# A hybrid decoder layer in float32: the order of three groups of weight loads and the run length of two stores

## The chip, the cores and the metric

The kernel runs on one core of a Trainium2 chip. The metric is the device time of one execution in microseconds (us): the median over several runs. Each run also has a span, from the first to the last instruction, and a granted TensorE clock. The engines are named as in the profile: PE (TensorE, matmuls), PEld (its weight loads), DVE (VectorE), ACT (ScalarE), POOL (GpSimd) and SP (SyncE, which here only issues transfers). ACT and POOL issue transfers too. An "L" with a number is a line of the kernel.

## The reference

One layer of a decoder, all in float32, for 2048 tokens of width 1024: a mixer (retention and pooling heads), cross-attention into 256 memory tokens, and a gated MLP, each with a norm in front and a residual add behind. What matters here, cut to the core:

```python
mem_n = rmsnorm(mem, mem_norm_g)
h = rmsnorm(x, mix_norm_g[l])
q, k, v, g, u = jnp.split(h @ w_in[l], [R, 2 * R, 3 * R, 4 * R], axis=-1)
y_ret = jax.nn.silu(g) * head_rmsnorm(retention(q, k, v, positions), ret_gn_g[l])
y_pool = pool_mixer(u, pool_w[l], pool_scale[l])
x = x + jnp.concatenate([y_ret, y_pool], axis=-1) @ w_out[l]
x = x + cross_attn(rmsnorm(x, xa_norm_g[l]), mem_n, xa_wq[l], xa_wkv[l], xa_wo[l])
x = x + conv_glu_ffn(rmsnorm(x, ffn_norm_g[l]), ffn_w_up[l], ffn_conv_w[l], ffn_conv_b[l], ffn_w_down[l])
...
# in cross_attn
q = h @ wq
k, v = jnp.split(mem_n @ wkv, 2, axis=-1)
s = (q k^T) * (XA_HEAD_DIM ** -0.5); p = softmax(s); o = p v
return o @ wo
# in pool_mixer: 4 groups of 128 channels
out = jnp.einsum('bsgc,gcd->bsgd', pooled, w); return out * scale
```

## The kernel before

**Precision.** Each float32 operand is split into a high part (float32r, rounded by an ACT copy) and a low part (the difference, on DVE): `split` (L256), or `pairs` (L285) for a block of weights in two halves. A product is three matmuls, high x high, high x low and low x high: `passes` (L269, matmuls at L271 to L273). So before any matmul of a block stand its load, two ACT copies (L259, or L262 with a gain) and two DVE subtractions (L243, L251).

**Buffers.** Raw blocks of 128 x 1024 land in five slots used in turn, `raws` (three in the tile R, two in tiles S). `new_raw` takes the slot that has been free longest and frees it in the program at once, so the next load into it waits for the splits of the block before. Halves go to `prs` (tile Q, and regions of G or E lent to it for a time). Slots in Z, eight of 128 x 1024, are taken with `Z.take(n)`, which picks the aligned group that was freed longest ago. TensorE's results go to PSUM banks (`mm`, five of them).

**Order of work.** The program is written in the order of its stages. A scheduler then fixes the order on each engine and each queue from that order and its own timing of the program; each engine then takes its list in that order and waits where an operand isn't there. Side work is a generator, `folded_weights` (L439), of which `folded(n)` (L2010) runs n steps at a place. Its steps:
1. Eight for the keys of the memory tokens and eight for their values (`project`, L480; the values are kept in the DRAM tensor Vd).
2. Four, one for each head: rows of `xa_wq` (wqT, two blocks of 512 KB, `row_pairs` at L495) times the keys give a score matrix, stored to the DRAM tensor Md (L548, L501).
3. One that loads poolT and the first rows of the output projection's pool half (wout_p, L497).
4. Two steps with one "pool product" each, then one with two more and the loads of Vd: pool weights times rows of wout_p, four groups g, each copied from two PSUM banks (L592) into a slot of Z and stored to the DRAM tensor WPd (L594) in runs of 128 values (512 B). The groups 2 and 3 take again the slots of groups 0 and 1.
5. Eight "half items" (`at` 0 to 7, L612): the values of a head times a half of its rows of `xa_wo` (two loads, L569, for each head; taken two half items ahead), copied with a scale (L633) and stored to the DRAM tensor VWd (L634), two stores of 256 KB a half item, in runs of 512 B.

**Stages for the first 1024 tokens.** The loop at L2021 runs steps 1 and 2 beside the loads of tokens (L658, L669). In its last four turns it also loads the weights of the retention values, w_v, 512 KB each (`value_weights`, L730, called at L2035 ahead of `folded(1)`), two into arena 0 (G, where the operands of the memory tokens had been) and two into arena 1 (E). `values` (L739) then uses them, and `quarter_sums` and `head_projections` follow; step 3 and the first two pool products lie in the last items of the head projections (L1886, L1888). After those come `folded(2)` (L2079: the last two pool products, then half item 0) and `folded(1)` for each remaining step of the last head's retention (L2081). Then the eight "output units" begin (L2116). Unit n loads wout_r[n] (L2118) and WPd[n] (L2119) into the two halves of a raw slot; the second half of its matmuls needs the latter. After the units 0, 1 and 2 run 1, 2 and 4 further steps (L2128).

Of the kernel before, what the change touches and what calls it, by code (L numbers as in the profile page):

```python
# [11 lines left out]
AF = mybir.ActivationFunctionType  # L12
# [3 lines left out]
P = 128  # L16
D = 1024
KT = D // P
SEQ = 2048
NMEM = 256  # L20
T = 1024
SUB = 512
# [114 lines left out]
def trunk(ctx, tc, xT, xR, memT, pos, w_qkgu, w_v, wkv, wqT, wo, wout_r, wout_p, poolT, w_up, w_dn, vecs, consts, outT):  # L137
    nc = tc.nc
    pe, act, dve, pool, sp = nc.tensor, nc.scalar, nc.vector, nc.gpsimd, nc.sync
# [11 lines left out]
    G = cp.tile([P, 28 * T], F32R, tag="G", name="G")  # L151
    X = G[:, : 2 * KT * T].rearrange("p (j t) -> p j t", t=T)

    def new_e(dtype):
        return Arena(cp.tile([P, 4 * T], dtype, tag="E", name=nm("E")), 0, 4, T)
# [4 lines left out]
    B = Joined(Arena(G, 16 * T, 12, T), new_e(F32R))  # L160

    def new_z(dtype):
        return Arena(cp.tile([P, 8 * T + 4 * EDGE], dtype, tag="Z", name=nm("Z")), 0, 8, T)

    Z = new_z(F32)
# [53 lines left out]
    VWd = drp.tile([KT, P, KT, P], F32, tag="VWd", name="VWd")  # L219
# [3 lines left out]
    WPd = drp.tile([KT, P, 4, P], F32, tag="WPd", name="WPd")  # L223

    def mmps():
        return mmp.tile([P, SUB], F32, tag="mm", name=nm("mm"))
# [42 lines left out]
    def passes(ps, lhs, rhs, start, stop, more=False):  # L269
        (lh, ll), (rh, rl) = lhs, rhs  # L270
        pe.matmul(ps, lh, rh, start=start, stop=False, skip_group_check=more)  # L271
        pe.matmul(ps, lh, rl, start=False, stop=False, skip_group_check=more)  # L272
        latest[0] = pe.matmul(ps, ll, rh, start=False, stop=stop, skip_group_check=more)  # L273
# [30 lines left out]
    def lend(region):  # L304
        for i in range(region.n):
            prs.freed.append(len(prs.one))
            prs.one.append(Arena(region.arena.t, region.arena.base + (region.first + i) * T, 1, T))

    def reclaim(region):
        for _ in range(region.n):  # L310
            prs.one.pop()
            prs.freed.remove(len(prs.one))
        region.free()
# [125 lines left out]
    def folded_weights():  # L439
# [18 lines left out]
        for k in range(KT):  # L458
            h, j = divmod(k, 4)
# [6 lines left out]
        rn = smp.tile([P, 4], F32, tag="rnm", name="rnm", bufs=1)[:, :2]  # L466
# [13 lines left out]
        def project(n):  # L480

            if n < 2:
                hs = first[0] if n == 0 else pairs(first[1])
            else:
                hs = pairs(load_tile(wkv[n]))
            if n % 2 == 0:
                bank[:] = [mmps()]
            at = n % 2 * NMEM
            ps = bank[0][:, at : at + NMEM]
            for k in range(KT):  # L490
                w = [hs[k // 4][:, i, (k % 4) * P : (k % 4 + 1) * P] for i in range(2)]
                passes(ps, w, (mh[:, k], ml[:, k]), k == 0, k == KT - 1)
            return ps

        def row_pairs(src):  # L495
            raw = new_raw()
            sp.dma_start(raw, src)  # L497
            return pairs(raw)
# [5 lines left out]
        def tiles4(d, nh, k):  # L504
            return d[4 * nh : 4 * nh + 4, :, k, :].rearrange("n p c -> p n c")
# [3 lines left out]
        ps = [project(n) for n in range(2)]  # L509
        sp.dma_start(cs_t, consts)  # L510
        memory_norm()
        for n in range(KT):
            if n > 1:
                ps.append(project(n))
            if n % 2:
                for at in (n - 1, n):
                    t = TT.take()
# [6 lines left out]
        for n in range(KT):  # L524
            ps.append(project(KT + n))
            if n % 2:
                del ps[:]
                t = TT.take()
# [7 lines left out]
        for h in range(HEADS):  # L536
            dp = [row_pairs(wqT[(2 * h + dt) * P : (2 * h + dt + 1) * P, :]) for dt in range(2)]
            for k2 in range(KT // 2):
                ps = mmps()
                for j in range(2):  # L540
                    for dt in range(2):
                        k = 2 * k2 + j
                        w = [dp[dt][k // 4][:, i, k % 4 * P : (k % 4 + 1) * P] for i in range(2)]
                        passes(ps[:, j * NMEM : (j + 1) * NMEM], w, (kp4[:, 2 * h + dt, 0], kp4[:, 2 * h + dt, 1]), dt == 0, dt == 1)
                t = TT.take()
                for j in range(2):
                    k = 2 * k2 + j
# [18 lines left out]
        def rows(h):  # L566
            got = [raws.take() for _ in range(2)]
            for dt, r in enumerate(got):
                sp.dma_start(r.f, wo[(2 * h + dt) * P : (2 * h + dt + 1) * P, :])  # L569
            return got  # L570
# [7 lines left out]
                    r.free()  # L578
            return out

        vp4, held = G[:, 8 * T : 12 * T].rearrange("p (n i m) -> p n i m", i=2, m=NMEM), []
        ended = []
        for g in range(4):
            u = ahead.pop(0)
            if g < 2:
                held.append(Z.take())
            t = held[g % 2]
            for nh in range(2):
                ps = mmps()
                lh = [pw.r[:, i * SUB + g * P : i * SUB + (g + 1) * P] for i in range(2)]  # L590
                passes(ps, lh, [u[nh][:, i] for i in range(2)], True, True)
                done = act.activation(t.f[:, nh * SUB : (nh + 1) * SUB], ps, AF.Copy)  # L592
            ended.append(done)
            act.dma_start(WPd[:, :, g, :].rearrange("n p c -> p n c"), t.f.rearrange("p (n c) -> p n c", n=KT))  # L594
            if g > 1:
                t.free()
            if g == 0:
                prs.freed.sort(key=lambda i: i < 3)
                ahead.append(row_pairs(wout_p[3]))
                got = rows(0)  # L600
            if g < 2:
                yield
# [9 lines left out]
        for at in range(2 * HEADS):  # L612
            h, nh = divmod(at, 2)
            dp = ahead
            if at == 2:
                reclaim(spare)
                spare = [Arena(G, at_g * T, 2, T).take(2) for at_g in (12, 6)]
                for r in spare:
                    lend(r)
                prs.freed.sort(key=lambda i: i < 3)  # L620
            if at + 1 < 2 * HEADS:
                with tc.issue_after((ended[-1] if at else ended[2]).ins):
                    ahead = halved(got, 1 - nh)
                if not nh and h + 1 < HEADS:
                    got = rows(h + 1)
            t = Z.take()
            for mt in range(2):
                ps = mmps()
                for dt in range(2):
                    lh = [vp4[:, 2 * h + dt, i, mt * P : (mt + 1) * P] for i in range(2)]  # L630
                    passes(ps, lh, [dp[dt][:, i] for i in range(2)], dt == 0, dt == 1)
                out = t.f[:, mt * SUB : (mt + 1) * SUB]
                ended.append(act.activation(out, ps, AF.Identity, scale=rn[:, mt : mt + 1]))  # L633
                act.dma_start(tiles4(VWd, nh, 2 * h + mt), out.rearrange("p (n c) -> p n c", n=4))  # L634
            t.free()
            yield
        for r in reversed(spare):
# [92 lines left out]
    def value_weights(kp, home=None):  # L730
        raw = new_raw()
        sp.dma_start(raw.rearrange("p (k n) -> p k n", k=2), w_v[2 * kp : 2 * kp + 2].rearrange("k p n -> p k n"))
        u = (home or B).take(2)
        for i in range(2):
            r = raw[:, i * SUB : (i + 1) * SUB]
            split(r, u.r[:, i * T : i * T + SUB], u.r[:, i * T + SUB : (i + 1) * T])
        return u
# [1272 lines left out]
    def folded(n):  # L2010
        for _ in range(n):
            next(todo, None)
# [4 lines left out]
    room, wv = [Z.take() for k in range(KT)], []  # L2017
# [3 lines left out]
    for n in range(1, 2 * KT + HEADS):  # L2021
        if n <= KT:
            load_tokens(0, n - 1, room)
        if 1 < n <= KT + 1:
            token_squares(0, n - 2, room, token_sums)
        if n == KT + 2:
            rn, _ = token_norm(token_sums[:, :KT])
        if n in xs_at:
            load_x_wide(xs_at[n], room)
        if n == 2 * KT:  # L2030
            reclaim(spare)
            spare = B.arenas[0].take(4)
            lend(spare)
        if 2 * KT <= n < 2 * KT + 4:
            wv.append(value_weights(n - 2 * KT, B.arenas[(n - 2 * KT) // 2]))  # L2035
        folded(1)
    reclaim(spare)
    for b in range(NB):

# [33 lines left out]
        if b:  # L2073
            parts = [next(heads)]
        else:
            slow[0], paced[0], spacing[0] = False, True, 7
            for _ in heads:
                pass
            folded(2)  # L2079
            for _ in behind[0]:  # L2080
                folded(1)  # L2081
            paced[0] = False
        mix = got[1]

# [31 lines left out]
        for n in range(first, KT):  # L2116
            raw = new_raw()
            sp.dma_start(raw[:, :SUB], wout_r[n].rearrange("p k c -> p (k c)"))  # L2118
            fetched[0] = sp.dma_start(raw[:, SUB:], WPd[n].rearrange("p k c -> p (k c)"))  # L2119
            got, ahead = ahead, fetch_x(b, n + 1) if n + 1 < KT else None  # L2120
            if not b:
                room.append(Z.take())
                load_tokens(1, n, room)
            unit(raw, mixed, add_residual(b, n, xs, got=got), (0, 1, 2, 4, 6, 7, 5, 3) if b == 0 else range(KT))
            if not b:
                token_squares(1, n, room, token_sums[:, KT:])
                room[n].free()
                folded((1, 2, 4, 0, 0, 0, 0, 0)[n])  # L2128
        paced[0] = True
        for u, _ in mix:  # L2130
            if u is not None:
# [8 lines left out]
        Z = new_z(F32)  # L2140
# [22 lines left out]
        for n in range(KT):  # L2163
# [9 lines left out]
            if n == KT - 1 and b + 1 < NB:  # L2173
                finish()
                wv = []
# [155 lines left out]
```

## Time and profile before

| | |
|---|---|
| median of 3 runs | 2416.39 us (2414.9 to 2418.16) |
| profiled execution, time | 2421.08 us |
| its span | 2419.3 us |
| its granted TensorE clock, mean | 0.997 |
| PE busy | 2390.1 us, 99% |
| DVE busy | 1734.0 us, 72% |
| ACT busy | 1350.3 us, 56% |
| bytes moved | 511.53 MB, mean 211 GB/s |

The profile's page is of one execution. Busy times are summed over the span; matmuls are pipelined and their ends are modelled, so a gap between two of them shows as idle time only where it is longer than that overlap. A row of the timeline has the start, the duration, the engine, the line and operation, out<-in with the tiles' names, and in brackets the idle time of the engine before it and what ended it. A row of the waits has who waited for whom, the us in total, how many times, and the longest. A letter q behind an engine's name is its sequencer, which issues transfers. In the rows of DMA issues the last figure is the time from issue to landing; the rows of DMA queues give packets, MB and the share of 16 engines' time in the window.

### The profile page before, as it was taken

What the parts mean: (1) busy time and instruction counts of PE and PEld (TensorE: products, weight loads), DVE (VectorE), ACT (ScalarE), POOL (GpSimd) and SP (SyncE); (2) the same over time, 40 slices, a digit from 0 to 9 for tenths busy, and PEclk for the clock granted to TensorE, in tenths of its full rate; (3) what the DMA queues carried; (4) which work ended last, traced back from release to release, by engine and by line L of the source; (5) the groups of instructions that cost most, each with busy time, mean ns of one, the idle gap of its engine ahead of it and who ended that gap; (6) DMA issues with size and microseconds to landing.
All of it is one profiled execution on the core that took longest, in us unless ns stands there. A gap on an engine that the chain in (4) does not pass through costs nothing.

```text
span 2419.3 us, 33286 instructions
## 1 busy us (share of the span) xinstructions
PE 2390.1 (99%) x11186; PEld 1993.0 (82%) x11186; DVE 1734.0 (72%) x2904; ACT 1350.3 (56%) x2488; POOL 276.0 (11%) x437
## 2 busy tenths in 40 slices
PE   9999999999999999999999999999999999999998
PEld 8888878888888888888888888888888888887886
DVE  7787774754667665665789776987677698877876
ACT  7654564443445543434555555755555577676673
POOL 0010000063034444100001000110000000000000
PEclk9999999999999999999999999999999999999999
DMA  9732187499688799785477554765455479757952
GB/s 360 262 122 90 63 269 231 135 255 329 194 231 218 188 244 322 195 283 191 140 243 258 184 190 131 251 194 183 158 175 185 134 257 314 238 178 265 345 180 74
DMA packets 267451, 511.53 MB, mean 211 GB/s; under 512 B 29184, under 2 KB 58384, under 8 KB 267280
## 3 DMA queue, kind: packets, MB, share of 16 engines
q1 hardware_dynamic: 209312, 402.30, 50.1%
q0 software_dynamic: 32768, 77.61, 13.1%
q10 hardware_dynamic: 25200, 29.49, 3.5%
q8 instruction: 88, 1.44, 0.2%
q14 instruction: 83, 0.68, 0.1%
HBM read 397.61 MB, written 180.89 MB: 239 GB/s over the span
## 4 chain that ended last, share of the span: by engine, by line
PE 94%; DMA 2%; ACT 2%; DVE 1%; issue 0%; SPq 0%; ACTq 0%; DVEq 0%
PE mm L271 29%; PE mm L272 29%; PE mm L273 29%; PE aux L271 1%; PE aux L273 1%; PE aux L272 1%; ACT G L259 1%; PE aux L901 1%; DMA WPd<-Z 1%; PE aux L778 1%; DVE Z L243 1%; PE aux L806 1%; PE aux L790 0%; PE aux L808 0%; DMA R<-wkv 0%
## 5 line engine op out<-in xcount | busy, mean ns | idle before, releaser
L271 PE MATMUL mm<-G,Q 128*128 128x512 f32 (+1 forms) x1631 | 624.7, 384 | 6.9 <-ACT Q L259 2.7
L273 PE MATMUL mm<-G,Q 128*128 128x512 f32 (+1 forms) x1631 | 619.8, 383 | 0.8 <-DVE Q L243 0.8
L272 PE MATMUL mm<-G,Q 128*128 128x512 f32 (+1 forms) x1503 | 574.1, 382 | 0.2 <-DVE G L251 0.2
L272 PE MATMUL mm<-G,E 128*128 128x512 f32 (+1 forms) x1092 | 420.7, 385 | 0.0
L271 PE MATMUL mm<-G,E 128*128 128x512 f32 (+1 forms) x1092 | 419.2, 386 | 0.5 <-ACT E L259 0.5
L273 PE MATMUL mm<-G,E 128*128 128x512 f32 (+1 forms) x1092 | 418.4, 385 | 0.4 <-DVE E L243 0.4
L271 PEld LDWEIGHTS mm<-G,Q 128*128 128x128 f32 x1631 | 307.0, 188 | 69.2 <-ACT Q L259 4.0
L273 PEld LDWEIGHTS mm<-G,Q 128*128 128x128 f32 x1631 | 306.8, 188 | 60.6 <-DVE Q L243 1.8
L272 PEld LDWEIGHTS mm<-G,Q 128*128 128x128 f32 x1503 | 283.0, 188 | 53.5 <-DVE G L251 0.4
L243 DVE TENSOR_TENSOR Z<-Z,mm 128x512 f32<-128x512 f32 (+1 forms) x322 | 216.4, 676 | 124.6 <-PE mm L273 121.8
L251 DVE SCALAR_TENSOR_TENSOR Z<-Z,vecs 128x1024 f32<-128x1024 f32 x176 | 224.9, 1282 | 50.3 <-ACT Z L1134 48.0
L271 PEld LDWEIGHTS mm<-G,E 128*128 128x128 f32 x1092 | 205.3, 188 | 41.8 <-ACT E L259 0.7
L273 PEld LDWEIGHTS mm<-G,E 128*128 128x128 f32 x1092 | 205.3, 188 | 41.8 <-DVE E L243 0.7
L272 PEld LDWEIGHTS mm<-G,E 128*128 128x128 f32 x1092 | 205.3, 188 | 41.0
L1071 ACT ACTIVATE E<-R 128x512 fp32r<-128x512 f32 (+1 forms) x165 | 101.6, 616 | 146.9 <-PE mm L272 138.7
L243 DVE TENSOR_TENSOR Q<-R,Q 128x512 fp32r<-128x512 f32 x174 | 119.0, 688 | 53.0 <-ACT Q L259 34.7
L243 DVE TENSOR_TENSOR T<-T 128x512 f32<-128x512 f32 (+4 forms) x189 | 130.0, 692 | 23.4 <-ACT T L432 12.0
L243 DVE TENSOR_TENSOR G<-T,G 128x512 fp32r<-128x512 f32 (+1 forms) x173 | 113.8, 678 | 32.4 <-ACT G L1018 18.9
L1018 ACT ACTIVATE G<-T 128x512 fp32r<-128x512 f32 x186 | 111.8, 623 | 36.5 <-DMA T<-Gd 28.6
L1134 ACT ACTIVATE Z<-Z,vecs 128x1024 f32<-128x1024 f32 x88 | 109.2, 1242 | 31.8 <-DVE Z L243 30.8
L1071 ACT ACTIVATE E<-S 128x512 fp32r<-128x512 f32 (+1 forms) x107 | 65.9, 616 | 108.8 <-PE mm L272 106.9
L243 DVE TENSOR_TENSOR E<-R,E 128x512 fp32r<-128x512 f32 (+1 forms) x133 | 89.3, 675 | 43.8 <-ACT E L1071 43.1
(348 smaller groups left out, 3948.3 us busy)
## 6 DMA issues: line engine op xcount, KB each, us to landing
T<-Gd SPq DMA_DIRECT2D x173, 256.0 KB, 4.3
Ud<-w_up POOLq DMA_DIRECT2D x132, 256.0 KB, 9.1
Gd<-Z SPq DMA_DIRECT2D x110, 256.0 KB, 2.6
R<-Ud SPq DMA_DIRECT2D x106, 256.0 KB, 2.8
R<-w_up SPq DMA_DIRECT2D x80, 256.0 KB, 3.1
S<-Ud SPq DMA_DIRECT2D x70, 256.0 KB, 2.9
Gd<-T SPq DMA_DIRECT2D x56, 256.0 KB, 3.3
S<-w_up SPq DMA_DIRECT2D x52, 256.0 KB, 3.1
```

The costliest lines, as they stand in the source:

```text
L243: return eng.tensor_tensor(out=out, in0=a, in1=b, op=op)
L251: return dve.scalar_tensor_tensor(out=out, in0=a, scalar=s, in1=b, op0=op0, op1=op1)
L259: one = act.activation(hi, src, AF.Copy)
L271: pe.matmul(ps, lh, rh, start=start, stop=False, skip_group_check=more)
L272: pe.matmul(ps, lh, rl, start=False, stop=False, skip_group_check=more)
L273: latest[0] = pe.matmul(ps, ll, rh, start=False, stop=stop, skip_group_check=more)
L778: pe.matmul(col(sc, c), self.ch(k, c), self.ch(q, c), start=True, stop=True)
L806: pe.matmul(col(y, c), col(self.pr.f, c), self.ch(v, c, h * T), start=True, stop=self.cur[c] is None)
L901: pe.transpose(tp[:, j * P : (j + 1) * P], e.f[:, j * P : (j + 1) * P], ident)
L1018: one = act.activation(hi, x, AF.Copy, scale=-1.0 if i == 2 else 1.0)
L1071: act.activation(p2[:, 0, :w], self.raw[i].f[:, :w], AF.Copy)
L1134: act.activation(self.c[g].f, a[:, 2:], AF.Identity, bias=cb[:, f : f + 1], scale=cw[2][:, f : f + 1])
```

## The change

Three edits:
1. **Value weights.** `value_weights` moves behind `folded(1)` in the loop at L2021, and by one turn: none in the turn of head 0, the first after head 1's step, the second after head 2's, the third and fourth after head 3's.
2. **Pool products and half items.** Groups 0 and 1 take a slot of Z each and free it at once; groups 2 and 3 take two adjacent slots together, interleaved, and leave in one store of 1 MB with runs of 256 values (1 KB). A half item interleaves its two results in its slot and stores them in one transfer of 512 KB with runs of 1 KB, once both are copied.
3. **Order ahead of the output units.** `folded(2)` instead of `folded(1)` in the loop over the rest of the last head's retention, so half items 0, 1 and 2 come before unit 0 (before: 0 and 1); after the units 0, 1 and 2 run 2, 2 and 2 steps (before: 1, 2 and 4).

```diff
-        vp4, held = G[:, 8 * T : 12 * T].rearrange("p (n i m) -> p n i m", i=2, m=NMEM), []
-        ended = []
+        vp4, ended = G[:, 8 * T : 12 * T].rearrange("p (n i m) -> p n i m", i=2, m=NMEM), []
         for g in range(4):
             u = ahead.pop(0)
-            if g < 2:
-                held.append(Z.take())
-            t = held[g % 2]
+            if g < 3:
+                held = Z.take(1 + g // 2)
+                t = held.f.rearrange("p (n k c) -> p n k c", n=KT, c=P)
             for nh in range(2):
...
-                done = act.activation(t.f[:, nh * SUB : (nh + 1) * SUB], ps, AF.Copy)
+                done = act.activation(t[:, 4 * nh : 4 * nh + 4, g % (held.n)], ps.rearrange("p (n c) -> p n c", c=P), AF.Copy)
             ended.append(done)
-            act.dma_start(WPd[:, :, g, :].rearrange("n p c -> p n c"), t.f.rearrange("p (n c) -> p n c", n=KT))
-            if g > 1:
-                t.free()
+            if g != 2:
+                act.dma_start(WPd[:, :, g + 1 - held.n : g + 1, :].rearrange("n p k c -> p n k c"), t)
+                held.free()
...
-                out = t.f[:, mt * SUB : (mt + 1) * SUB]
-                ended.append(act.activation(out, ps, AF.Identity, scale=rn[:, mt : mt + 1]))
-                act.dma_start(tiles4(VWd, nh, 2 * h + mt), out.rearrange("p (n c) -> p n c", n=4))
+                out = t.f.rearrange("p (n k c) -> p n k c", n=4, c=P)
+                ended.append(act.activation(out[:, :, mt], ps.rearrange("p (n c) -> p n c", c=P), AF.Identity, scale=rn[:, mt : mt + 1]))
+            act.dma_start(VWd[4 * nh : 4 * nh + 4, :, 2 * h : 2 * h + 2, :].rearrange("n p k c -> p n k c"), out)
             t.free()
...
-        if 2 * KT <= n < 2 * KT + 4:
-            wv.append(value_weights(n - 2 * KT, B.arenas[(n - 2 * KT) // 2]))
         folded(1)
+        for kp in {2 * KT + 1: (0,), 2 * KT + 2: (1,), 2 * KT + 3: (2, 3)}.get(n, ()):
+            wv.append(value_weights(kp, B.arenas[kp // 2]))
...
             for _ in behind[0]:
-                folded(1)
+                folded(2)
...
-                folded((1, 2, 4, 0, 0, 0, 0, 0)[n])
+                folded((2, 2, 2, 0, 0, 0, 0, 0)[n])
```

## The prediction

> **What bounds the kernel.** I read the page's busy times and its chain first, then the TensorE waits and the granted clock stage by stage, then each wait back to the transfer behind it.
>
> ```profile
> span 2419.3 us, 33286 instructions
> PE 2390.1 (99%) x11186; PEld 1993.0 (82%) x11186; DVE 1734.0 (72%) x2904; ACT 1350.3 (56%) x2488; POOL 276.0 (11%) x437
> ...
> PE 94%; DMA 2%; ACT 2%; DVE 1%; issue 0%; SPq 0%; ACTq 0%; DVEq 0%
> ```
>
> TensorE is the bound: 99% busy and 94% of the chain. The change removes no matmul, so it can only win time in which TensorE waits or runs at a lower clock. Two stages that it touches have some: the stage that makes the score matrix from the query rows (near 64 us) and the stretch before the first output unit (326 to 348 us). Their waits, one answer for each:
>
> ```profile
> PE mm L271 <- ACT G L259: 3.4, 2, 2.2
> ```
>
> ```profile
> PE mm L271 <- ACT Q L259: 2.0, 2, 1.3
> PE mm L271 <- ACT Z L592: 0.6, 1, 0.6
> PE mm L271 <- ACT Z L633: 0.6, 1, 0.6
> PE mm L271 <- DVE T L243: 0.5, 1, 0.5
> ```
>
> So 3.4 us lie in the first stage, 3.7 us in the second. The windows (length, then busy us of PE, PEld, DVE, ACT, POOL, granted clock, DMA share, GB/s) add what the clock takes:
>
> ```profile
> 58.00:82.00 24.00, 20.57 (x166) 19.96 (x166) 17.21 (x26) 22.86 (x49) 0.00 (x0) 1.00 0.89 304
> ...
> 335.00:338.00 3.00, 1.72 (x8) 0.88 (x6) 3.00 (x7) 2.84 (x6) 0.00 (x0) 1.00 1.02 342
> 338.00:340.00 2.00, 1.41 (x5) 0.93 (x5) 2.00 (x5) 2.00 (x7) 0.00 (x0) 0.66 1.08 347
> 340.00:342.00 2.00, 2.00 (x9) 1.69 (x8) 1.79 (x3) 2.00 (x7) 0.00 (x0) 0.50 1.14 343
> 350.00:400.00 50.00, 50.00 (x222) 41.38 (x221) 20.94 (x32) 24.67 (x45) 0.00 (x0) 1.00 0.85 283
> ```
>
> After TensorE was busy for only 1.72 of 3 us, its clock fell to 0.66 and 0.50. That costs (1 - 0.66) x 1.41 + (1 - 0.50) x 2.00 = 1.5 us. From 350 to 400 us nothing is lost, and the last row gives the pace: 50/222 = 0.225 us a matmul.
>
> **Part one, the value weights behind the query rows.**
>
> ```profile
> 44.55 0.38 SPq L732 DMA_DIRECT2D R<-w_v  x1
> 45.83 0.33 SPq L497 DMA_DIRECT2D R<-wqT  x1
> ...
> 70.70 1.53 SPq L497 DMA_DIRECT2D R<-wqT  x2
> ```
>
> ```profile
> 56.69 0.63 ACT L259 ACTIVATE G<-R 128x512 fp32r<-128x512 f32 x1 [1.55 <-PE mm L273]
> 57.23 1.14 ACT L259 ACTIVATE Q<-R 128x512 fp32r<-128x512 f32 x2
> ...
> 66.00 0.67 ACT L259 ACTIVATE G<-R 128x512 fp32r<-128x512 f32 x1
> ```
>
> Each load takes the next of five raw slots in turn, and a slot is free once both halves are split on ACT and DVE. The first value weights occupy one from 44.55 us, but their home still holds the memory operands of the matmuls, so their split on ACT waits 1.55 us (row 56.69), and behind it in ACT's order the query rows wait. Before the split that TensorE lacks (66.00) stand four value halves: 4 x (57.23 - 56.69) = 2.2 us of ACT. With the 1.55 that is 3.7 us, more than the longest wait of 2.2; two more halves (1.1 us) stand before the second, shorter one. ACT is busy 22.86 of 24 us here, so its order decides. All eight query loads move up on SP and the four value loads behind them; after those come the token loads of the next stage, at the same place.
>
> Bounds: 3.4 us (all waits) and 0 (DMA share 0.89, so the loads might come no sooner). Could the values stage wait for its weights instead? The landing times of the eight query loads, of the same size, and its first matmul:
>
> ```profile
> DMA to landing us min/median/max: 4.6/5.7/6.1
> ```
>
> ```profile
> 86.07 0.40 PE L271 MATMUL mm<-G 128*128 128x512 f32 x1
> ```
>
> The last value load would leave about where the last query load leaves now (70.70 + 1.2), land 6.1 later and, with two halves on ACT and two on DVE (2.2), be ready at 80.2. The stage would begin at 86.07 - 3.3 = 82.8 and wants the third and fourth pair only 24 matmuls (5.4 us) later. So 8 us cover it; beyond them each us late would cost one. I take 3.3, by the ACT rows. The moved instructions themselves cost what they cost now.
>
> **Part two, longer runs and another slot.** The chain of waits:
>
> ```profile
> 319.72 6.53 DMA R<-Vd
> ...
> 326.33 1.06 ACT G L259
> 327.39 0.48 ACT Z L592
> ...
> 327.90 7.24 DMA WPd<-Z
> ...
> 335.66 0.59 ACT Z L592
> ...
> 336.28 5.61 DMA WPd<-Z
> ...
> 341.98 5.39 DMA R<-WPd
> ...
> 348.07 0.49 PE mm L271
> ```
>
> ```profile
> 320.91 0.61 ACT L592 ACTIVATE Z<-mm 128x512 f32<-128x512 f32 x1
> ...
> 335.16 0.60 ACT L592 ACTIVATE Z<-mm 128x512 f32<-128x512 f32 x1 [1.59 <-DMA WPd<-Z]
> ```
>
> The fourth pool product is copied into the slot of the second, whose store lands at 335.14; ACT stands 1.59 us and holds up the split for the first output unit (TensorE's 1.3 us) and the VW copies (L633, 0.6 us). After the change the third and fourth go into a pair of slots that the code took from the last head's key and value, read long before. Gains: 1.3 + 0.6, and with those waits most of the 1.5 of the clock: 3.4.
>
> Costs. (a) The first product frees its slot at once, and as the longest free it goes to the second product. The first store:
>
> ```profile
> WPd<-Z ACTq DMA_DIRECT2D x1, 512.0 KB, 7.6
> ```
>
> It leaves at 319.48 by ACT's list and lands at 327.1, so the copy of 320.91 moves there. Queued behind it on ACT are the splits of Vd and, for their banks, TensorE's third and fourth products. If the splits are ordered in front, the second copy moves from 327.39 by one copy, 0.5; if behind, they move from 324.4 to 327.7, 3.3. ACT is idle before them anyway:
>
> ```profile
> ACT G L259 <- DMA S<-Vd: 2.9, 1, 2.9
> ```
>
> So most of the shift falls into that idle time, and I take 0.9.
> (b) The joined store is complete only after the fourth copy, at 336.28 - 1.59 = 334.7, and carries 1 MB. The queue rows, 331 to 342 us (512 B runs, WPd and VWd) and 68 to 85 us (1 KB, Md):
>
> ```profile
> q10 hardware_dynamic: 4425, 2.22, 67.3%
> ```
>
> ```profile
> q10 hardware_dynamic: 2160, 2.08, 34.9%
> ```
>
> A packet took 0.673 x 16 x 11 / 4425 = 26.8 ns and 0.349 x 16 x 17 / 2160 = 43.9 ns: twice the bytes in 1.64 times. The store takes 5.61 to 5.61 x 1.64 = 9.2 us and lands at 340.3 to 343.9 (now 341.89); the unit's second half could start 1.6 earlier to 2.0 later. I take 0, because another half item is ready to fill (below). The Trainium skill, "DMA: Bandwidth & Descriptors", section Specifications, gives 512 B as enough for line rate. By that rule, against the rows, the joined store takes 2 x 5.61 = 11.2 us, the unit comes up to 4.0 later, and the sum shrinks by 1.3 beyond the 2.7 of one half item. The VWd stores fall from 16 to 8, likewise in 1 KB runs, and the first half now waits for the second copy. Its first reader comes long after:
>
> ```profile
> L353 SPq DMA_DIRECT2D S<-VWd x8: 320/330/341, 443.6 to 1060.2; - x8
> ```
>
> TensorE loses nothing while those stores run (350 to 400), so they bring 0. The spaced copies write as many elements: 0, bounds -0.1 and +0.1 each for those in the stalled stretch.
>
> **Part three, three half items in front.** A half item is 12 matmuls x 0.225 = 2.7 us. Work is only moved, but so are its loads:
>
> ```profile
> 328.68 0.33 SPq L2118 DMA_DIRECT2D R<-wout_r  x1
> ...
> 332.71 1.39 SPq L569 DMA_DIRECT2D R<-wo  x2
> ```
>
> The third half item brings the next two wo rows in front of the unit's wout_r in the ring: they take the slot of 328.68 and that of 332.71, and wout_r gets the last, at about 333.4 (332.71 plus half of the row). At 5.4 to 6.5 us (rows of this stretch) it lands near 339.3, and with 0.6 of splitting the unit starts at 340.0 instead of 336.8. TensorE has the third half item from about 335.5 to 338.2, so up to 1.8 is open; ending transposes and a fourth half item, whose rows land about 338, can fill part. Bounds 0 and 1.8; I take 0.8. Later units get two half items each instead of 1, 2 and 4: free, as TensorE loses nothing there.
>
> On the clock: the longest wait here was 1.3 us, and still it fell to 0.50. The Trainium skill, "TensorE: Matmul & The Clock Gate", Part 1, asks for an idle window of about 3.4 us. The trace does not agree. By the page my remaining 0.8 leaves the clock full; by the trace it may halve it again, and then 1.5 of the gain is gone.
>
> **Sum.** -3.3 - 3.4 + 0.9 + 0.8 = -5.0 us. The profiled execution took 2421.08 us, its span and 1.8 around it; the median of the runs shown, 2416.39, lies 4.7 lower, and I take the difference off that: 2411.4.
>
> **Rivals.** *All is filled*: the fourth half item covers every gap, costs (a) and the open 0.8 vanish, and of the 2.0 the last 0.7 goes too: -3.3 - 3.4 - 0.7 = -7.4, 2409.0. For it, a row of the third half item, which already stands in the unit's gap:
>
> ```profile
> 345.36 0.40 PE L271 MATMUL mm<-Q,G 128*128 128x512 f32 x1
> ```
>
> *First stage alone*: the unit's weights come late by as much as ACT gains: -3.3, 2413.1. For it: DMA share above 1.0 from 335 on. *Query rows come no sooner* (the reordering does not do what it says): -1.7, 2414.7; against it, the ACT rows. *Slower*: at the second product ACT waits on its own store with the Vd splits behind it. All that follows on ACT is 3.3 late, the joined store leaves at 338.0 and lands at 343.6 to 347.2, up to 5.3 behind now, and at that end the 3.4 is not won: +5.3 - 3.3 = +2.0, 2418.4. It decides once the delay costs over 3.3, and for more than 0.2% it must cost over 8.1. Against it: 2.9 us of ACT idle already at Vd.
>
> **How the numbers follow.** Forecast 0.45, all filled 0.20, first stage alone 0.17, query rows no sooner 0.08, slower 0.10. A measurement tells about 0.2%, 4.8 us, from no change. The forecast straddles it: somewhat over half of its 0.45 (0.25), the 0.20 and 0.02 of the third make faster 0.47. Slower by that much is half of the slower case, should the late store also disturb the order of later stages, and 0.01 of the third: 0.06. Same is the rest, 0.47. The likeliest case alone spans 2408.5 to 2414; from a full gain with the clock (2407) to the slower case (2417), the range leaves out less than 2 in 10.
>
> **What would show it.** Right: no TensorE wait near 64 to 70 us, value splits behind 66 us, no ACT wait for WPd at the fourth product, three WPd and eight VWd stores. Wrong: ACT waiting at the second product for a WPd store, a clock of 0.50 again near 340, wout_r issued after 333 with TensorE waiting for it, or TensorE waiting for value weights near 82 us.

## The result: slower by 0.3%, and the profile after

| | before | after |
|---|---|---|
| median of 6 runs each | 2416.96 us (2414.9 to 2419.83) | 2425.36 us (2423.47 to 2426.22) |
| profiled execution, time and span | 2421.08, 2419.3 us | 2423.47, 2421.7 us |

The ratio is 1.0033 (95% interval 1.0020 to 1.0046): 8.4 us slower, where 5 us faster were forecast (8.0 us by the ratio). The profiled execution of after is the fastest of its six, that of before is slower than all of its six, so the two spans show only 2.4 us of it.

The page of after: the span, the busy times and the queue that takes the WPd and VWd stores.

```profile
span 2421.7 us, 33287 instructions
PE 2393.4 (99%) x11186; PEld 1996.3 (82%) x11186; DVE 1735.1 (72%) x2904; ACT 1350.0 (56%) x2488; POOL 278.0 (11%) x437
...
q10 hardware_dynamic: 19936, 29.49, 3.4%
```

The work is the same, and the same 29.49 MB go in 19936 packets (before: 25200, so the runs are longer). Behind the edit of the pool products a line of after has a number one lower than in before: L815 is the L816 of before, L591 its L592. The windows of after (columns as in the prediction), then those windows of before that the prediction does not show:

```profile
60.00:84.00 24.00, 23.76 (x185) 22.77 (x184) 15.62 (x23) 23.12 (x52) 0.00 (x0) 1.00 0.97 344
140.00:152.00 12.00, 10.00 (x43) 7.66 (x42) 9.49 (x18) 4.43 (x7) 0.54 (x1) 1.00 0.48 138
292.00:308.00 16.00, 13.12 (x50) 9.99 (x49) 9.23 (x21) 12.02 (x26) 0.00 (x0) 0.79 0.22 66
312.00:352.00 40.00, 37.30 (x184) 29.39 (x183) 35.80 (x76) 29.21 (x70) 0.00 (x0) 1.00 0.80 262
894.00:906.00 12.00, 9.33 (x36) 7.31 (x35) 6.64 (x11) 4.02 (x7) 6.71 (x11) 0.86 1.07 341
```

```profile
140.00:152.00 12.00, 11.74 (x52) 9.34 (x52) 10.69 (x22) 5.31 (x8) 0.54 (x1) 1.00 0.35 113
292.00:308.00 16.00, 14.59 (x78) 11.73 (x77) 12.03 (x24) 15.26 (x32) 0.00 (x0) 1.00 0.28 83
312.00:352.00 40.00, 36.28 (x168) 28.06 (x167) 32.48 (x69) 26.18 (x63) 0.00 (x0) 0.96 0.91 298
894.00:906.00 12.00, 12.00 (x55) 9.93 (x54) 9.03 (x15) 5.66 (x12) 7.10 (x12) 1.00 1.07 310
```

The two stretches that were to gain did: the first is full but for 0.24 us, and the second (before: 36.28 of 40 at a clock of 0.96) waits less and keeps its clock. The loss lies in places that the change does not touch: at 140, near 250 (one wait of 1.2 us), at 300 and, some 500 us behind the last half item, at 900. TensorE's waits in after, one view for each place (at 64 us, 140, 296 and 898):

```profile
PE mm L271 <- ACT G L259: 0.2, 1, 0.2
```

```profile
PE mm L271 <- DVE T L243: 1.3, 1, 1.3
PE mm L273 <- DVE S L243: 0.7, 1, 0.7
```

```profile
PE aux L820 <- ACT T L815: 2.0, 1, 2.0
```

```profile
PE mm L271 <- ACT Q L259: 2.7, 1, 2.7
```

From here on a balance helps. Each matmul's start, with the matmuls ahead of it summed by their width, gives the time at which two executions have done equal work. The differences to the profiled execution of before in us, at the times of before in the head of the table (one execution each; the labels are explained below):

| kernel | 94 | 144 | 150 | 256 | 326 | 363 | 894 | 904 |
|---|---|---|---|---|---|---|---|---|
| after | -2.8 | -2.8 | -0.8 | +0.4 | +4.0 | +1.4 | +1.4 | +5.7 |
| edit one alone (p1_values) | -2.8 | -2.8 | -0.4 | +0.9 | +4.1 | +2.0 | +3.0 | +3.0 |
| edit three alone (p4_order) | +0.6 | +0.6 | +0.5 | +0.5 | +0.6 | +0.4 | +1.5 | +6.0 |
| Q's list turned (q_turned) | +0.6 | +0.6 | +0.5 | +0.4 | +0.5 | -0.1 | 0.0 | +4.4 |
| edit one, tables earlier (p1_tables) | -2.2 | -2.2 | -1.5 | -1.6 | -1.4 | -2.1 | -2.0 | -2.0 |
| pairs and joined stores (v22_joined) | -3.1 | -3.1 | -3.6 | -3.7 | -3.8 | -6.6 | -6.6 | -6.6 |

After is ahead by 2.8 us until 144. It loses 2.0 by 150, 1.2 by 256 and 3.6 by 326 (the wait of 2.0 at 296 and a half clock behind it), takes 2.6 back by 363 (1.7 of these are a stretch of half clock that this execution of before had there) and loses 4.3 at 898.

### The profile page after: what moved, and what is told of

Same layout as the page of the kernel before. It is cut to its first block, busy times and chain, and to the rows that moved or that the text cites. A ratio compares the mean times of both kernels' runs of the same rounds, so it can differ in the third digit from the quotient of the medians.

```text
span 2421.7 us, 33287 instructions
## 1 busy us (share of the span) xinstructions
PE 2393.4 (99%) x11186; PEld 1996.3 (82%) x11186; DVE 1735.1 (72%) x2904; ACT 1350.0 (56%) x2488; POOL 278.0 (11%) x437
## 3 DMA queue, kind: packets, MB, share of 16 engines
q10 hardware_dynamic: 19936, 29.49, 3.4%
## 4 chain that ended last, share of the span: by engine, by line
PE 94%; ACT 2%; DVE 2%; DMA 1%; issue 1%; SPq 0%; ACTq 0%; DVEq 0%
PE mm L271 30%; PE mm L272 29%; PE mm L273 29%; DVE Z L243 1%; PE aux L777 1%; PE aux L900 1%; PE aux L271 1%; PE aux L272 1%; PE aux L273 1%; PE aux L789 1%; PE aux L805 0%; PE aux L807 0%; ACT G L259 0%; PE aux L363 0%; DMA Xd<-T 0%
```

## The experiments

All ratios are to runs of the kernel before taken beside them on the same chip, with 95% intervals; medians of different tables come from different chips, so across tables the ratios are compared. Where a label starts with p or v, the kernel is the one before with the edits named.

### Each edit alone

```diff
# p1_values: edit one;  p2_products: edit two, pool products;  p3_joined: edit two, half items
# p4_order: edit three
-                folded(1)
+                folded(2)
...
-                folded((1, 2, 4, 0, 0, 0, 0, 0)[n])
+                folded((2, 2, 2, 0, 0, 0, 0, 0)[n])
```

> Edit one alone (value weights behind the query rows), all else as before. Comparing the two profiled executions at equal work of TensorE, the changed kernel is 4.1 us ahead at 70 us, 2.8 ahead from 80 to 141 and 0.8 ahead at 150; it falls behind only at 296 to 309 (4.5 us) and at 898 to 904 (4.3 us). Theory A: the late losses belong to edits two and three (slots, half items, row loads); then this kernel is at -0.8 us, no change that can be measured, about 2416, with no TensorE wait near 298 and 898. Rival B: the earlier queries shift the scheduler's own timing of all that follows, and the late losses come with this edit: +5 to +8 us, 2422 to 2425, with waits near 298 and 898.

> The pool-product half of edit two alone: groups 0 and 1 free their slot at once, 2 and 3 go as a pair in one store. Theory A (prediction's own terms): the ACT wait of 1.6 us at the fourth copy goes, a shorter one comes at the second; -1 to -3 us, 2414 to 2416. Rival B: taking a pair and freeing slots early turns the order in which Z slots are freed, so later stages that take slots meet other waits: +2 to +5 us.

> The half-item part of edit two alone: each half item stores its two results in one transfer of 512 KB in 1 KB runs. Theory A: nothing waits for these stores, 0 +-1 us, about 2417. Rival B: eight fewer instructions on ACT's queue and another timing in the scheduler shift the order from 330 us on, +2 to +4 us, with new waits behind 340 us.

> Edit three alone: three half items ahead of unit 0, then 2, 2 and 2. Theory A: the third half item's two row loads and its splits come into the last head's retention, and the unit loads of both halves of the tokens use other raw slots: the losses at 296 to 309 and at 898 to 904 come with this edit, +4 to +9 us, 2421 to 2426. Rival B: the half item fills the wait ahead of the unit (-1 to -2 us) and the late losses belong to another edit, 2415 to 2416.

| | median us | ratio |
|---|---|---|
| p1_values | 2420.86 | 1.0020 (1.0012 to 1.0029) |
| p2_products | 2417.50 | 1.0004 (0.9995 to 1.0013) |
| p3_joined | 2415.05 | 0.9999 (0.9989 to 1.0008) |
| p4_order | 2424.37 | 1.0032 (1.0019 to 1.0044) |

Edits one and three are slower each by itself; the two halves of edit two can't be told from no change, and for p2_products neither theory's range was met. For p1_values theory A missed, and rival B held in part: the losses at 143, 250 and 296 come with edit one alone, but not the one at 898, and the 4.4 us lie below its range. For p4_order the time lies in the range of theory A; of its two places only 898 is right. So there are two causes. The four ratios add up to 1.0055, the whole change has 1.0033; with intervals of about 0.001 on each side of every one the two are barely apart, and why they don't add was not tried.

### The losses of edit one: the order behind it

The timeline of before at 127 to 141 us, then that of edit one alone: the rope tables' table load on ACT, and DVE's products with the tables.

```profile
127.80 1.28 ACT L724 ACT_TABLE_LOAD   x1
...
138.19 1.29 DVE L243 TENSOR_TENSOR Z<-Z,T 128x512 f32<-128x512 f32 x2 [3.09 <-DMA Z<-rope]
```

```profile
129.74 0.60 ACT L1723 ACTIVATE E<-mm 128x512 f32<-128x512 f32 x1 [2.03 <-PE mm L273]
130.23 0.62 ACT L1708 ACTIVATE Q<-R 128x512 fp32r<-128x512 f32 x1
130.87 1.28 ACT L724 ACT_TABLE_LOAD   x1
...
142.94 1.29 DVE L243 TENSOR_TENSOR Z<-Z,T 128x512 f32<-128x512 f32 x2 [3.05 <-DMA Z<-rope]
```

TensorE is 2.8 us earlier, yet the table load is 3.1 us later: it now stands behind a copy (L1723) that waits 2.03 us for TensorE. The tables go out to DRAM and come back, so DVE's products are 4.75 us later (138.19 to 142.94) and TensorE waits behind DVE. At 296 us it is the same kind of thing, the last operations ahead of a head's scaling (L816), before and with edit one alone:

```profile
294.36 0.22 DVE L247 TENSOR_SCALAR sm<-sm,consts 128x8 f32<-128x8 f32 x1
...
294.86 2.15 ACT L816 ACTIVATE T<-aux,sm 128x128 f32<-128x128 f32 x8
```

```profile
296.05 1.15 ACT L259 ACTIVATE G<-Z 128x512 fp32r<-128x512 f32 x2 [0.21 <-PE mm L272]
...
296.39 0.23 DVE L247 TENSOR_SCALAR sm<-sm,consts 128x8 f32<-128x8 f32 x1
...
297.23 1.21 ACT L1739 ACTIVATE R<-mm 64x512 f32<-64x512 f32 x2
...
298.46 1.91 ACT L816 ACTIVATE T<-aux,sm 128x128 f32<-128x128 f32 x7
...
298.88 1.50 PE L821 MATMUL aux<-consts,T 128*128 128x128 f32 x5 [1.96 <-ACT T L816]
```

The small operation that ends the scale is 2.0 us later on DVE, and after it the scalings still stand behind two further splits and two copies on ACT. None of these instructions is in the diff. The scheduler fixed their order by its own timing of the program, in which the stages now begin at other times. The traces let one count the places: among ACT's operations and table loads, the rope tables' load and the first scaling of the heads 0, 1 and 2 are the numbers 162, 227, 282 and 323 in before, and 165, 232, 284 and 327 in edit one alone, in after and in after_q (below). In every other kernel here the scalings stand at the places of before.

Two runs put the value weights elsewhere, chosen so that the written order keeps the table load and the scalings at the places of before:

```diff
# v112        {2 * KT + 1: (0,), 2 * KT + 2: (1, 2), 2 * KT + 3: (3,)}
# v112_joined: the same, with p3_joined's edit
```

> Edit one alone in another placing: the first value weights behind head 1's step, the second and third behind head 2's, the fourth behind head 3's (in the change: one, one, then two). The queries move ahead as in the change; what differs is the order that the scheduler writes for ACT and DVE afterwards: in the change the rope tables' table load, the scalings at L816 and the small operations ahead of them stand 3 to 5 places later on ACT than before, in this kernel at the places of before. Theory A (the early gain is given back by that order, not by the earlier queries): the 4.1 us at 70 us stay in part to the end, no new waits at 143 to 147, 250 and 296; -2.5 to -4.5 us, 2412 to 2414. Rival B (the later stages can't start sooner whatever their order, since rope loads and DVE set their time): the gain is given back by 150 us and the time is that of before within 1 us.

> The same placing with the joined half-item stores beside it, the pool products and the order ahead of the units as before. If the parts add (A): about 1.5 to 3 us below the kernel with the placing alone, 2409 to 2412, and so faster than before and than the change. If the joined stores' 3.4 us at 315 to 325 came only from the order of that stage, which the earlier queries may turn again (B): no gain beside the placing alone, 2412 to 2417.

v112: 2417.34 us, 1.0003 (0.9994 to 1.0012). v112_joined: 2415.30 us, 0.9996 (0.9987 to 1.0005). The waits at 250 and 296 are back to those of before and the one at 143 is 0.8 us (before 0.3), much as A says, and yet there is no gain: with three value loads ahead of the last two query loads, TensorE waits 1.8 us for the latter at 77. Neither theory held whole. Two pairs keep the order and put two value loads ahead, as the change does:

```diff
# v22         {2 * KT + 2: (0, 1), 2 * KT + 3: (2, 3)}
# v22_joined: the same, with p3_joined's edit
```

> The value weights in two pairs, behind head 2's and behind head 3's step, with the joined half-item stores; all else as before. The placing one, two, one put three value loads ahead of the last two query loads, and TensorE waited 1.8 us for them at 77; here two stand ahead, as in the change. Theory A: 2.8 us ahead from 70 to 141 us, as in the change, and since the order on ACT is that of before, at most 1 us of it goes at 147 and none at 250 and 296: 1 to 2 us below the kernel with one, two, one, 2412.5 to 2414.5. Rival B (what is ahead at 141 is given back at 147 whatever is done, since the rope loads set the time): no better than the joined stores alone, 2415 to 2416.

> The value weights in two pairs behind head 2's and head 3's step, nothing else changed. If the 3.1 to 3.7 us of its placing are kept and the joined stores gave the rest (A): 2412.5 to 2414.5, 1 to 2 us above the kernel with joined stores. If the joined stores do nothing (B): 2412 within 0.7 us.

v22: 2412.93 us, 0.9985 (0.9976 to 0.9995). v22_joined: 2411.99 us, 0.9985 (0.9975 to 0.9994), where v112_joined has 0.9996. The early gain is kept to the end (last row of the balance). Whether the joined stores add to it is not settled; the intervals are nearly the same.

These placings differ from that of the change in loads as well as in order. The next kernel keeps the change's placing and turns the order back by another edit:

```diff
             if place[0] > 2:
                 next(tables, None)
+            if place[0] > 5:
+                next(tables, None)
```

> Edit one with the change's own placing of the value weights, and one line that traces the steps of the rope tables earlier (two steps instead of one in each of the last three turns of the values stage). With it the scheduler's order on ACT has the rope table load and the scalings of all heads at the places of before. Theory A (edit one alone lost its gain to the order written behind it): the 2.8 us of 80 to 141 us are kept to the end, no waits at 143, 250 and the longer one at 296: 5 to 7 us below edit one alone (2420.9), 2413.5 to 2416. Rival B (the placing itself, with its later value loads, costs the gain): within 1.5 us of edit one alone, above 2419.

> The change's own placing with the rope tables' steps earlier and the joined half-item stores. If the parts add (A): 1 to 2 us below the kernel without the joined stores, 2412 to 2414.5, faster than before. If not (B): as that kernel.

> The kernel before with only the line that traces the rope tables earlier. Theory A (the line only restores the order that the early queries turned): within 1.5 us of before, 2414.5 to 2417.5. Rival B (earlier tables gain by themselves, and p1_tables' gain is theirs): 2 to 4 us faster, 2412 to 2414.

| | median us | ratio |
|---|---|---|
| p1_tables: edit one and this line | 2413.02 | 0.9987 (0.9979 to 0.9996) |
| p13_tables: with the joined stores too | 2412.42 | 0.9983 (0.9974 to 0.9992) |
| before_tables: this line alone | 2418.28 | 1.0013 (1.0004 to 1.0022) |

```profile
128.33 1.28 ACT L724 ACT_TABLE_LOAD   x1
...
138.51 1.29 DVE L243 TENSOR_TENSOR Z<-Z,T 128x512 f32<-128x512 f32 x2
```

In the timeline of p1_tables the table load and the products are back near the times of before, the table load and the scalings have the numbers 161, 227, 282 and 323, and edit one alone falls from 1.0020 to 0.9987, some 8 us. Not all of it is won back: TensorE still waits 0.9 us at 143 (before 0.3). The line alone gains nothing; it costs 3.1 us by the ratio (1.0 to 5.3), more than either theory expected, so the gain is edit one's own. That the order behind the edit took the gain back is thus shown.

### The loss at 898 us: a free list

A half of a block of weights is split into one of three slots in Q (`prs`), and the slot is the one first in a list of free slots. Edit three leaves this list, and that of the raw slots, in another rotation at the start of the second 1024 tokens. The edits of three kernels in one cut:

```diff
     for b in range(NB):
+        if b:
+            prs.freed[:] = [1, 2, 0]          # p4_ring, with the next line
+            raws.freed[:] = [1, 2, 0, 3, 4]   # p4_ring_raws: alone
+            prs.freed[:] = [2, 0, 1]          # q_turned, in the kernel before
```

> Edit three alone, and at the start of the second half the free lists of the raw slots and of the slots for halves in Q are set to the order that they have there before the change ([1, 2, 0, 3, 4] and [1, 2, 0]; edit three alone leaves [1, 2, 3, 4, 0] and [2, 0, 1]). Theory A (the wait of 2.8 us at 898 us and the half clock behind it come from the turned free lists): both go, and the time falls by about 4.3 us against edit three alone, to 2419 to 2421. Rival B (they come from transfers that were moved in time by the earlier stages): the wait stays, 2423 to 2425.

> As the kernel before it, but only the raw slots' free list is set back, that of Q's slots stays turned. If the raw slots decide which weights load late at 898 us (A): the wait goes here too, 2419 to 2421. If Q's slots decide it, by the order in which ACT splits and frees them (B): the wait of about 2.8 us stays, 2423 to 2425.

> The kernel before with one line more: at the start of the second half the free list of Q's slots is set to [2, 0, 1], as edit three leaves it, where it would be [1, 2, 0]. Nothing is added or taken away; in the lists of the engines only a handful of instructions of the second half's weights (wout_r, WPd) and their splits change places. Theory A (this list alone makes the wait of 2.8 us at 898 us and the half clock behind it): +4.3 to +7 us, 2420 to 2423, with the wait at 898 and without any change before 850 us. Rival B (it needs the other moves of edit three too): within 1 us of before.

| | median us | ratio |
|---|---|---|
| p4_ring: edit three, both lists set back | 2417.22 | 1.0005 (0.9996 to 1.0013) |
| p4_ring_raws: only the raw slots' | 2423.28 | 1.0026 (1.0016 to 1.0036) |
| q_turned: before, Q's list turned | 2422.10 | 1.0023 (1.0012 to 1.0034) |

Q's list is the cause: setting back the raw slots alone keeps the wait (2.9 us), and turning Q's list in the kernel before, with not one operation or transfer more or less on any engine (the page counts four instructions more, semaphore instructions of DVE and SP), costs 5.6 us by the ratio. The ACT rows of q_turned:

```profile
885.87 0.63 ACT L259 ACTIVATE Q<-R 128x512 fp32r<-128x512 f32 x1 [0.84 <-PE aux L272]
...
891.59 0.63 ACT L259 ACTIVATE Q<-R 128x512 fp32r<-128x512 f32 x1 [0.24 <-ACT aux L427]
...
898.15 0.33 ACTq L865 DMA_DIRECT2D Xd<-T  x1
898.52 0.60 ACT L427 ACTIVATE aux<-T 128x512 f32<-128x512 f32 x1 [2.68 <-DMA T<-xT]
899.06 0.61 ACT L259 ACTIVATE Q<-R 128x512 fp32r<-128x512 f32 x1
```

and TensorE's wait in it:

```profile
PE mm L271 <- ACT Q L259: 2.6, 1, 2.6
```

Behind the three units that run first in the second half, the list is made anew as [0, 1, 2], so the half that unit 3 needs first goes to slot 0. With the list of before, slot 0 is long free and this half is split first of the three. With the turned list, slot 0 holds the last weights of the three units, and the scheduler splits the other two halves first, at 885.87 and 891.59 (the addresses in the two programs, which no trace shows, tell which is which). The needed one is third, at 899.06, behind a store of residuals and an ACT operation that waits 2.68 us for tokens. The kernel v22_joined with the third rotation:

> The fastest kernel so far (value weights in two pairs, joined stores) with Q's free list in the third of its three rotations, [0, 1, 2], at the start of the second half. The rotation of before has no wait at 898, the one of edit three a wait of 2.7. If one rotation alone is bad (A): as without the line, 2412 within 1 us. If only that of before is good (B): 2 to 6 us slower, with a wait near 895.

2412.77 us, 0.9983 (0.9975 to 0.9992), no wait at 895: of the three rotations one is bad, as far as tried (the third in this kernel alone).

### The whole change with its two orders mended

> The whole change, with the free list of Q's slots set back to [1, 2, 0] at the start of the second half. If the turned list adds in the whole change what it adds to edit three alone (A): 4.3 to 7 us less than the change, 2418 to 2421, no wait near 898. If the wait at 898 comes in the whole change from late transfers as well (B): less than 2 us less, above 2423.

> The whole change with the two lines altered that the runs so far blame: the value weights in two pairs behind head 2's and head 3's step, and the free list of Q's slots set back at the start of the second half. Theory A (the later order after the early queries, and the turned list, are what made the change slower): 2414 to 2417, at least 7 us below the change, no new waits at 250, 296 and 898. Rival B (the order of the stage at 300 to 350 us, with a third half item and new slots, costs by itself): 2418 to 2421.

> The whole change with two lines more: the rope tables' steps traced earlier, as in p1_tables, and the free list of Q's slots set back at the start of the second half. Theory A (the two orders are the whole loss): 10 to 12 us below the change, 2413 to 2415.5, no waits at 143, 250 and 898. Rival B (edits two and three cost by themselves as well): 2416 to 2419.

| | median us | ratio to before |
|---|---|---|
| after_q: Q's list set back | 2419.39 | 1.0015 (1.0006 to 1.0024) |
| mended: that, and the value weights in two pairs | 2413.99 | 0.9993 (0.9984 to 1.0002) |
| after_tables_q: Q's list, and tables earlier | 2416.62 | 1.0002 (0.9993 to 1.0011) |

By the ratios Q's list is worth 4.3 us in the whole change (1.0033 to 1.0015), and the order behind edit one another 3.1 (after_tables_q) or 5.3 (mended). With after_tables_q that is 7.5 of the loss of 8.0 us, the whole of it within the intervals. Yet theory A of after_tables_q (2413 to 2415.5) missed, and 2416.62 lies in the range of its rival B: the gain of 3 us that p1_tables keeps is not there. What is missing to it lies in edits two and three: after_tables_q is 4.6 us by the ratio above p13_tables, which lacks the new slots of the pool products and the third half item, and mended 1.9 us above v22_joined, which lacks the same two. TensorE's waits from 312 to 352 us in the profiled execution of after_tables_q, 4.6 us where before has 3.7:

```profile
PE mm L271 <- ACT Z L632: 1.8, 1, 1.8
PE mm L271 <- DVE T L243: 1.3, 1, 1.3
PE mm L272 <- DVE G L243: 1.3, 1, 1.3
PE mm L271 <- ACT G L259: 0.2, 1, 0.2
```

Which of the two edits they belong to was not tried.

## Why the prediction was wrong

**Part one, -3.3 at its own stage: right there.** TensorE's wait fell from 3.4 to 0.2 us, and 2.8 us were won and held to 140 us. One reading of the edit was wrong, without harm: not all query loads move ahead of the value loads; in after two value loads (54.81 and 64.19 us) still leave ahead of the last two queries (66.72 and 68.57). The values stage did not wait for its weights. With the order of before kept, v22 and p1_tables bring it to the end: 0.9985 and 0.9987, or 3 to 4 us.

**The step that failed is "The moved instructions themselves cost what they cost now", and the sum that lets -3.3 stand to the end.** It took the lists of all engines behind the moved loads as fixed. They were written again, with the scalings up to five places later on ACT: edit one alone measured +4.4 us instead of -3.3.

**Part two, -3.4 with +0.9 and 0: not borne out in the time.** The change of slots did what was foreseen. The timeline of after:

```profile
323.91 0.37 ACTq L594 DMA_DIRECT2D WPd<-Z  x1
...
330.01 1.09 ACT L591 ACTIVATE Z<-mm 128x512 f32<-128x512 f32 x2 [0.82 <-DMA WPd<-Z]
```

The second product's copy waits for the first store (0.82 us), the fourth for none. But the pool products alone measured 1.0004 and the joined half-item stores 0.9999, so the -2.5 of the sum was too much. The joined WPd store of p2_products (transfer, KB, us from issue to landing) and TensorE's waits there from 312 to 352 us:

```profile
WPd<-Z ACTq DMA_DIRECT2D x1, 1024.0 KB, 9.0
```

```profile
PE mm L271 <- ACT Q L259: 2.0, 1, 2.0
PE mm L271 <- DVE T L243: 1.4, 1, 1.4
PE mm L271 <- ACT Z L591: 0.7, 1, 0.7
PE mm L271 <- ACT Z L632: 0.3, 1, 0.3
```

The store took 9.0 us, the upper of the two bounds (5.61 and 9.2) in (b), and landed at 344.3. The load of the unit's second half leaves behind it, and TensorE waits 2.0 us for that half where it waited 0.7 before. "I take 0, because another half item is ready to fill" was a mis-sized term: 1.3 us in this execution. The waits of 1.3 (for the first unit's split) and 0.6 that were to go did go, but the wait for DVE at 331 us rose from 0.5 to 1.4, so the waits came to 4.4 us in all where before has 3.7. In after the store took 7.0 and no such wait shows. Nor was the 1.5 us of half clock a sure gain: it isn't in every execution (below).

**Part three, +0.8: the local term was in its bounds, its mechanism was not as told, and the far term was missing.** The two wo rows were to leave in front of wout_r, and wout_r at 333.4. SP's rows of after, then of p4_order:

```profile
329.96 0.82 SPq L569 DMA_DIRECT2D S<-wo  x2
332.97 0.33 SPq L2117 DMA_DIRECT2D R<-wout_r  x1
336.25 1.01 SPq L569 DMA_DIRECT2D R<-wo  x2
```

```profile
328.91 0.33 SPq L569 DMA_DIRECT2D R<-wo  x1
330.72 0.33 SPq L2118 DMA_DIRECT2D R<-wout_r  x1
332.94 0.33 SPq L569 DMA_DIRECT2D R<-wo  x1
```

In after wout_r leaves ahead of both rows, as in before, and it leaves at 332.97 because the whole stage runs 4 us later; that this is near 333.4 is luck. With edit three alone one row stands in front and wout_r is 2.0 us later than before, not 4.7. TensorE's waits from 312 to 352 us in that execution add up to 3.9 us (before 3.7), and with the lists set back edit three can't be told from no change (1.0005). "Later units get two half items each ... free" looked at TensorE alone; the same steps take and free the slots of the lists from which a stage 500 us later is written. That is 4.3 to 6.5 us by the ratios in the three comparisons (after_q, q_turned, p4_ring).

**The rival on the slower side** put the loss at the second product's copy. The place was wrong; ACT's waits there came to 0.8 us in after and 1.0 in p2_products. A disturbed order of later stages is named once, beside the chance for slower, as a thing that a late store might bring; it has no price, and none of the rivals is a change of order or of a free list. Slower had 0.06.

## What to carry to other kernels

Where a scheduler writes the engines' lists from the program's order and its own timing, a moved load can change the order of instructions that it has nothing to do with, and a gain at its own place says little about the end; compare the written order of the later stages before trusting a local sum. Any list of free slots that outlives the edit is part of the edit: ask in which rotation it reaches the next stage that reads it. A gain that was given back can then be kept by another placing (0.9985) or by one line that puts the order back (0.9987).

## What the runs showed of the clock

Within an execution all half-clock stretches start on one grid of 3.413 us, whose phase differs from execution to execution. Before has them at 338.65 and 2209.16 us, which is 548 times 3.4133 apart. A count over all 20 profiled executions here, from that grid and TensorE's idle time in each window (the first windows and the end left out; ends of matmuls are modelled): of 17 windows with 1.6 us of idle time or more, all 17 were followed by a window at half clock; of 93 with 0.9 to 1.6 us, 12; of 13802 with less, none. So a wait of 2 us costs another 1.7 us where it falls into one window, and nothing more where a window's edge parts it. In the kernel before, the wait of 2.2 us at 64 left the clock full; in q_turned the same wait was followed by a half window. Two profiled executions of nearly the same program can differ by some us for this alone, so a row of the balance is good to about 2 us (an estimate from the 1.7), and the verdicts above rest on the medians and ratios.

The Trainium skill, "TensorE: Matmul & The Clock Gate", Part 1 ("What's actually happening"), gives a free-running window of 3413 ns, and these traces agree. It lets the clock fall after at least one idle window; here a window that was idle for 1.6 of its 3.4 us was enough.
